# First output projection of a hybrid decoder layer: the last two weight blocks taken tile by tile, its norm split in two steps, and the sample attention spread over another stretch

## The chip, the cores and the metric

One core of one Trainium2 chip runs the kernel; the seven others are idle. The metric is the device time of one execution in microseconds (us), as the median of several runs. Five engines work side by side, each through its own list of instructions in a fixed order: PE (TensorE, matmuls and transposes), DVE (VectorE), ACT (ScalarE), POOL (GpSimd) and SP (SyncE, which here only issues DMAs). An engine stops at an instruction whose inputs are not ready, and all that stands behind it in its list stops with it.

## What is computed

One layer of a hybrid decoder, for a prompt of 1024 tokens and for 8 samples of 8 new tokens over a paged cache of 512 positions. The model width is 1024, the feed-forward width 2816, and everything is float32.

```python
xn = rmsnorm(x, norm_mix_g)
z = xn @ w_in                       # columns of four head groups
mix = concatenate([y_lru, y_sc, y_fox, y_diff]) @ w_out
x = x + mix                         # "first output projection"
x = x + (silu(rmsnorm(x) @ w_gate) * (rmsnorm(x) @ w_up)) @ w_down
y = rmsnorm(x, norm_final_g)        # at the very end
```

`y_fox` is a forgetting attention and `y_diff` a differential attention (two softmaxes, the second subtracted with a weight lambda, then a norm over each head). For the samples both run over gathered cache pages plus the new rows. The change touches the multiplication by `w_out` for the first 512 prompt tokens, the RMSNorm behind it, and the order in which the sample attention is laid beside them.

## The kernel before

**Precision.** Every float32 product is made of three matmuls (`mm3`, L94 to L97): each operand is split into a high part and the rest, `whi` and `wlo` for a weight, `xTh` and `xTl` for an activation. A weight block of 1 MB is loaded by SP into a `raw` tile (a ring of three) and split in four parts of 128x512, each part by one ACT copy (`whi`, L326) and one DVE subtraction (`wlo`, L327), into a ring of eight pairs of tiles. `W.get` (L369) asks for a block and, while `W.ahead` is set, also starts the split of the next one, as far as the ring has room.

**Order of the work.** The program is a list of items, each a cost and a function that emits instructions. `merge(a, b, frac)` (L1255) interleaves two lists so that the share of cost done in both stays equal; with `frac` below 1 the second list is used up when that share of the first is done. The items are emitted in that order; the tile scheduler then sets the order on each engine and may place an instruction ahead of others that were emitted before it. `keep` (L86) marks an instruction as one to be kept in program order.

**The stage around the change** (about 340 to 500 us of the span). The first half of the prompt (four tiles of 128 tokens) has its mixed rows in `xTh`, `xTl`. `w_out_items` (L1596) multiplies them with `w_out` in four column blocks of 256: for block n, for each tile t, 24 matmuls of 256 columns into one of three `pb_mm` banks, then a DVE addition to the residual `acc[t]` (L1611). So the order is block by block, tile inside. `load_acc` (L1864) loads the four residual tiles of 512 KB each from the input with SP (L1869). Behind the projection `norm2_items` (L1876) runs `norm_T` (L440) on each tile: ACT squares and sums the row (`rstd_of`, L431), DVE makes one over the root from nine small operations (L433, L123, and three times L125 and L126), scales the tile into a `raw` tile (L443), PE transposes it in two lots of four (L450, banks `pb_t`, of which there are two), and ACT and DVE write the halves `xTh` (L452) and `xTl` (L453). The `raw` tile comes from the same ring of three as the weight blocks. Then the gate and up matmuls of the first feed-forward blocks run, merged with the second half's attention (`att_items`), which `att1_open` (L2011 to L2030) opens with its loads `aqt`, `afb`, `akt`, `avt`.

**The sample attention** (`sample_items`, L1341) is a second list, merged with the projection: 60% of its items over the projection behind its first items, the other 40% over the norm. In two groups (fox) and four groups (diff) it does: gather of K pages by POOL (`spgk`, L1406) and transposes (`kT`, L1424, copies L1426 and L1428), scores (`qk`, L1439), softmax on DVE and ACT (L1464 to L1482), transposes of the probabilities (`pT`, L1493, L1496, copies L1494, L1497), the product with V (`pv`, L1507, L1512, gathered `spgv`), a masked product that selects the rows (`som`, `sel`, L1522, L1526), and after each group kind `fin` (L1535 to L1556): for diff a sum (L1532), square, reduction and a root of some dozen small DVE operations, a scaling (L1548), and two transposes (L1551) whose results go to `syt` (L1554). `setup_c` (L1362) loads the constants `sc` and computes from them `ssg` (L1373), a 128x1 weight for diff's softmax; `setup_b` loads `sbias` and `snb`, from which POOL makes the bias (L1464).

The lines of the program that order all this are L2138 to L2150. In the changed kernel the same code stands some lines lower: L1373 is L1395, L1611 is L1616, L443 is L442, L450 is L453, L452 and L453 are L455 and L456, L1526 is L1531, L1548 is L1553, L1551 is L1556, L1554 is L1559, L1058 is L1064.

Of the kernel before, what the change touches and what calls it, by code (L numbers as in the profile page):

```python
# [8 lines left out]
F32 = mybir.dt.float32  # L9
# [32 lines left out]
P3_FRAC = .75  # L42
P3_SMP = 0.6
N1_FRAC = 0.6
# [21 lines left out]
def hybrid_step(ctx, tc, I, C, O):  # L66
# [370 lines left out]

    st_x = {}

    def norm_T(pool, x, gb, R, xh, xl, c0, act=False):  # L440
        xs = big(pool, "nxs", 2)[:R]
        y = rstd_of(x, xs, R, "n", act)  # L442
        st_x["x"] = nc.vector.scalar_tensor_tensor(xs, x, y[:R], gb[:R], op0=OP.mult, op1=OP.mult)  # L443
        kn = 512 // R
        for kk in range(8 // kn):
            pt = bank("t")
            pv = pt.rearrange("p (k r) -> p k r", r=R)
            for i in range(kn):
                k = kk * kn + i
                nc.tensor.transpose(pv[:, i, :], xs[:, k * 128:(k + 1) * 128], ident[:R, :R])  # L450
            ks = slice(kk * kn, (kk + 1) * kn)
            nc.scalar.activation(xh[:, ks, c0:c0 + R], pv, AF.Copy)  # L452
            nc.vector.tensor_tensor(xl[:, ks, c0:c0 + R], pv, xh[:, ks, c0:c0 + R].bitcast(F32), op=OP.subtract)  # L453
        if R == 64:
            nc.vector.tensor_copy(xh[:, :, c0 + 64:c0 + 128], xl[:, :, c0:c0 + 64].bitcast(F32))  # L455

    def xT_tiles(pool, smp):
# [883 lines left out]
    def sample_items(E_):  # L1341
# [20 lines left out]
        def setup_c():  # L1362
            sp = E_["sp"]
            t = sp.tile(list(CN["smp"].shape), F32, name="sc")
            nc.sync.dma_start(t, C["smp"])
            c = 0
            for nm, nf, nd in (("bm", 4, 4), ("sel", 128, 256), ("msk", 128, 256)):
                for key, n in (("f", nf), ("d", nd)):
                    S[nm + key] = t[:, c:c + n]
                    c += n  # L1370
            S["sgA"], S["sgB"] = t[:, c:c + 1], t[:, c + 1:c + 2]
            sg = sp.tile([128, 1], F32, name="ssg")
            nc.vector.scalar_tensor_tensor(sg, S["sgB"], nlam, S["sgA"], op0=OP.mult, op1=OP.add)  # L1373
            S["sg"] = sg
        def setup_b():
# [13 lines left out]
        def setup_d():  # L1389
            setup(False)  # L1390
            bd = S["bd"]
            S["bo"] = bo = E_["hp"].tile([128, 576], F32, name="sbo", tag="hTl", bufs=3)[:, :520]
# [203 lines left out]
    def w_out_items(hf, e):  # L1596
        items = []

# [16 lines left out]
        for n in range(4):  # L1615
            r = [f(n, t, c, kind) for t, c, kind in tok_tiles(hf)]  # L1616
            if hf == 0 and n == 0:
                items += sum((x[:3] for x in r[:3]), []) + sum((x[3:] for x in r[:3]), [])
                r = r[3:]
            items += sum(r, [])  # L1620
        return items

# [241 lines left out]
    def load_acc(pool, hf):  # L1864
        acc = []
        for t in range(4 + hf):
            a = pool.tile([128, D], F32, name=f"acc{t}")
            if t < 4:
                nc.sync.dma_start(a, I["x_prompt"][0, hf * HALF + t * 128:hf * HALF + (t + 1) * 128, :])  # L1869
            else:  # L1870
                nc.vector.memset(a[64:128], 0.0)
                nc.sync.dma_start(a[0:64], I["x_sample"].rearrange("s t d -> (s t) d"))
            acc.append(a)
        return acc

    def norm2_items(hf, e):  # L1876
        st = {}

        def f(t):
# [11 lines left out]
            return g  # L1891
        return [(900, f(t)) for t in range(4 + hf)]

    def final_items(hf, e):
# [82 lines left out]
    def do(f):  # L1977
        return [(0, f)]
# [164 lines left out]
    smp = SM_ITEMS[3:]  # L2143
    k = int(len(smp) * P3_SMP)
    wo = w_out_items(0, E2[0])
    prog += SM_ITEMS[:3] + wo[:WO_HEAD] + merge(wo[WO_HEAD:], smp[:k]) + merge(norm2_items(0, E2[0]), smp[k:]) + do(att1_open)
    prog += merge(head, att_items(A1, 1), P3_FRAC)
# [94 lines left out]
```

## Time and profile before

| | |
|---|---|
| median of 3 runs | 1378.14 us (1369.75 to 1383.42) |
| the profiled execution | 1374.64 us |
| its span, first to last instruction | 1372.9 us |
| PE busy | 1342.1 us (98%) |
| DVE busy | 1058.3 us (77%) |
| ACT busy | 675.7 us (49%) |
| mean DMA rate | 148 GB/s |
| mean granted PE clock | 0.993 |

The profile is of one execution; the span leaves out 1.7 us of it before the first and behind the last instruction. "Idle before" an instruction is the time its engine stood still, with what released it. A row with xN at the end is N instructions in one line.

### The profile page before, as it was taken

The numbers are of one execution on the slowest core, as the hardware profiler recorded it, in microseconds if no ns is written. First come the engines' busy times: TensorE is split into PE (matmuls) and PEld (weight loads), VectorE is DVE, ScalarE is ACT, GpSimd is POOL, SyncE is SP. The second block draws the span as 40 slices with busy tenths as digits, with TensorE's granted clock in tenths as the row PEclk, the third lists the DMA queues.
The fourth block names the chain that finished last, engine by engine and source line by source line (L and its number), as shares of the span: only waits on it lengthen the run. The fifth ranks groups of instructions, "written<-read, shape, count | busy, mean of one in ns | idle before, by whom it ended". The sixth has DMA issues, their size and how long they took to land.

```text
span 1372.9 us, 23083 instructions
## 1 busy us (share of the span) xinstructions
PE 1342.1 (98%) x8477; PEld 1182.0 (86%) x8477; DVE 1058.3 (77%) x2699; ACT 675.7 (49%) x1326; POOL 125.1 (9%) x154
## 2 busy tenths in 40 slices
PE   9899999999899999999999999999999999999997
PEld 8799897888786688888888999997999999999996
DVE  6776377798446568899969988548998888888885
ACT  6585466775233258655544444324534444444454
POOL 3101012311243011000000000000200000000001
PEclk9999999999999999999999999999999999999999
DMA  8656438676994376444236433612624333333311
GB/s 259 203 169 206 139 118 274 211 229 217 328 305 152 108 238 196 147 131 124 86 116 190 123 92 93 192 48 62 200 62 123 93 92 93 93 92 93 93 47 69
DMA packets 202866, 202.65 MB, mean 148 GB/s; under 512 B 16529, under 2 KB 165549, under 8 KB 202626
## 3 DMA queue, kind: packets, MB, share of 16 engines
q1 hardware_dynamic: 189568, 168.60, 40.3%
q0 software_dynamic: 7328, 25.11, 5.2%
q10 hardware_dynamic: 5858, 7.47, 1.5%
q8 instruction: 67, 1.10, 0.3%
q14 instruction: 45, 0.37, 0.1%
HBM read 170.56 MB, written 32.29 MB: 148 GB/s over the span
## 4 chain that ended last, share of the span: by engine, by line
PE 81%; DMA 7%; ACT 5%; DVE 4%; issue 1%; SPq 0%; POOL 0%; ACTq 0%; DVEq 0%; POOLq 0%
PE pb_mm L95 10%; PE pb_mm L96 10%; PE pb_mm L97 10%; PE pb_mm L1746 8%; PE pb_s L1746 5%; PE pb_t L1746 5%; PE pb_o L1162 2%; PE pb_t L95 2%; PE pb_s L97 2%; PE pb_t L96 2%; PE pb_o L1746 2%; PE pb_s L96 2%; PE pb_s L95 2%; PE pb_t L97 2%; PE pb_t L1142 2%; DMA raw<-in_w_in_dram 2%
## 5 line engine op out<-in xcount | busy, mean ns | idle before, releaser
L326 ACT ACTIVATE whi<-raw 128x512 fp32r<-128x512 f32 (+1 forms) x409 | 251.8, 629 | 353.1 <-PE pb_mm L97 75.6
L327 DVE TENSOR_TENSOR wlo<-raw,whi 128x512 fp32r<-128x512 f32 (+1 forms) x405 | 275.8, 692 | 71.6 <-ACT whi L326 62.9
L95 PE MATMUL pb_mm<-xTh,whi 128*128 128x512 f32 (+2 forms) x536 | 192.5, 359 | 1.7 <-ACT whi L326 1.5
L96 PE MATMUL pb_mm<-xTl,whi 128*128 128x512 f32 (+2 forms) x536 | 191.1, 357 | 0.3 <-DVE xTl L453 0.3
L97 PE MATMUL pb_mm<-xTh,wlo 128*128 128x512 f32 (+2 forms) x536 | 190.7, 356 | 0.3 <-DVE wlo L327 0.3
L97 PEld LDWEIGHTS pb_mm<-xTh,wlo 128*128 128x128 f32 x536 | 101.1, 189 | 13.9 <-issue 1.6
L95 PEld LDWEIGHTS pb_mm<-xTh,whi 128*128 128x128 f32 x536 | 101.2, 189 | 13.7 <-ACT whi L326 1.7
L96 PEld LDWEIGHTS pb_mm<-xTl,whi 128*128 128x128 f32 x536 | 101.3, 189 | 10.4 <-DVE xTl L453 0.5
L95 PE MATMUL pb_mm<-whi,xTh 128*128 128x256 f32 (+1 forms) x312 | 92.1, 295 | 4.9 <-DVE acc L1611 4.9
L96 PE MATMUL pb_mm<-wlo,xTh 128*128 128x256 f32 (+1 forms) x312 | 89.3, 286 | 0.0
L97 PE MATMUL pb_mm<-whi,xTl 128*128 128x256 f32 (+1 forms) x312 | 89.1, 286 | 0.0
L1100 ACT ACTIVATE aP<-aP,anm 128x128 f32<-128x128 f32 (+7 forms) x96 | 73.9, 770 | 30.0 <-DVE anm L1098 28.6
L1832 DVE TENSOR_TENSOR acc<-acc,pb_mm 128x512 f32<-128x512 f32 (+1 forms) x95 | 64.7, 681 | 15.1 <-PE pb_mm L97 13.2
L95 PE MATMUL pb_mm<-whi,hTh 128*128 128x512 f32 (+1 forms) x179 | 70.7, 395 | 0.1
L97 PE MATMUL pb_mm<-whi,hTl 128*128 128x512 f32 (+1 forms) x179 | 70.6, 394 | 0.0
L96 PE MATMUL pb_mm<-wlo,hTh 128*128 128x512 f32 (+1 forms) x179 | 70.3, 393 | 0.0
L95 PEld LDWEIGHTS pb_mm<-whi,xTh 128*128 128x128 f32 x312 | 60.0, 192 | 10.1 <-DVE acc L1611 5.1
L97 PEld LDWEIGHTS pb_mm<-whi,xTl 128*128 128x128 f32 x312 | 59.9, 192 | 0.6 <-issue 0.4
L96 PEld LDWEIGHTS pb_mm<-wlo,xTh 128*128 128x128 f32 x312 | 60.1, 193 | 0.4 <-DVE wlo L327 0.2
L1147 DVE TENSOR_TENSOR aAl<-pb_t,aAh 128x512 fp32r<-128x512 f32 (+1 forms) x80 | 49.1, 632 | 6.0 <-ACT aAh L1146 5.0
L1746 PE MATMUL pb_mm<-xTh,whi 128*128 128x288 f32 (+1 forms) x184 | 53.7, 292 | 0.0
L1746 PE MATMUL pb_mm<-xTh,wlo 128*128 128x288 f32 (+1 forms) x184 | 53.7, 292 | 0.0
(623 smaller groups left out, 3773.2 us busy)
## 6 DMA issues: line engine op xcount, KB each, us to landing
raw<-in_w_gate_dram SPq DMA_DIRECT2D x44, 512.0 KB
raw<-in_w_up_dram SPq DMA_DIRECT2D x44, 512.0 KB
raw<-in_w_down_dram SPq DMA_DIRECT2D x22, 1024.0 KB
raw<-in_w_in_dram SPq DMA_DIRECT2D x12, 1024.0 KB
raw<-in_w_in_dram SPq DMA_DIRECT2D x16, 512.0 KB
raw<-in_w_out_dram SPq DMA_DIRECT2D x8, 1024.0 KB
akt<-fkD SPq DMA_DIRECT2D x24, 256.0 KB
akt<-dkD SPq DMA_DIRECT2D x48, 128.0 KB
```

Of the source, the lines that this page charges most:

```text
L95: kp(nc.tensor.matmul(out, lhsT=lh, rhs=rh, start=first, stop=False))
L96: kp(nc.tensor.matmul(out, lhsT=lh, rhs=rl, start=False, stop=False))
L97: kp(nc.tensor.matmul(out, lhsT=ll, rhs=rh, start=False, stop=last))
L326: i1 = nc.scalar.activation(hi, s, AF.Copy)
L327: i2 = (nc.gpsimd if pool else nc.vector).tensor_tensor(lo, s, hi.bitcast(F32), op=OP.subtract)
L1100: nc.scalar.activation(dst[:, :ln], dst[:, :ln], AF.Exp, bias=nmx, accum_out=sm)
L1142: nc.tensor.transpose(pt[:, o:o + 128], P[ti][:, kb * 128:(kb + 1) * 128], ident)
L1147: nc.vector.tensor_tensor(al[:, :o], pt[:, :o], ah[:, :o].bitcast(F32), op=OP.subtract)
L1162: nc.tensor.matmul(po[:, q0:q0 + n], lhsT=v[:, kb, :], rhs=a[:, o:o + n], start=kb == 0 and i == 0, stop=kb >= nkb - 2 and i == 1, skip_gr ...
L1746: nc.tensor.matmul(pt, lhsT=w[:, k], rhs=x[:, k], start=first and k == 0 and i == 0, stop=k == 3 and i == 2, skip_group_check=True)
L1832: nc.vector.tensor_tensor(a, a, pt, op=OP.add)
```

## The change

Six things are done, all in the stage described.

1. `norm_T` is divided into `norm_a` (square, root, scaling, on ACT and DVE) and `norm_b` (transposes and copies).
2. Of the projection's four column blocks the first two stay as they were. The last two (`w2`, `w3`) are both kept split in the ring of eight and are taken tile by tile: tile 0 of both, then tile 1, and so on. After each tile its `norm_a` is emitted, and from tile 2 on `norm_b` of the tile two before. `W.ahead` is off meanwhile; the first gate and up block is split (`split_next`) in tile 3 between its two blocks.
3. `norm_b` of tiles 2 and 3 is emitted after the first gate and the first up group of the feed-forward; these two groups leave the list that is merged with the second half's attention.
4. The sample items are merged with the whole of this by 0.8: they are all emitted when eight tenths of its cost is.
5. `ssg` is computed in `setup_d` (the start of the diff groups), marked with `keep`, instead of in `setup_c`.
6. The four residual tiles are loaded in two column pieces each, first 256 columns of all four, then 768: eight DMAs instead of four.

```diff
-    def norm_T(pool, x, gb, R, xh, xl, c0, act=False):
+    def norm_a(pool, x, gb, R, act=False):
         xs = big(pool, "nxs", 2)[:R]
         y = rstd_of(x, xs, R, "n", act)
-        st_x["x"] = nc.vector.scalar_tensor_tensor(xs, x, y[:R], gb[:R], op0=OP.mult, op1=OP.mult)
+        nc.vector.scalar_tensor_tensor(xs, x, y[:R], gb[:R], op0=OP.mult, op1=OP.mult)
+        return xs
+    def norm_b(xs, R, xh, xl, c0):
...
         def setup_c():
...
-            sg = sp.tile([128, 1], F32, name="ssg")
-            nc.vector.scalar_tensor_tensor(sg, S["sgB"], nlam, S["sgA"], op0=OP.mult, op1=OP.add)
-            S["sg"] = sg
         def setup_d():
             setup(False)
+            sg = S["sg"] = E_["sp"].tile([128, 1], F32, name="ssg")
+            keep(nc.vector.scalar_tensor_tensor(sg, S["sgB"], nlam, S["sgA"], op0=OP.mult, op1=OP.add))
...
     def w_out_items(hf, e):
-        items = []
+        items, late = [], []
...
-            items += sum(r, [])
-        return items
+            if hf == 0 and n >= 2:
+                late.append(r)
+            else:
+                items += sum(r, [])
+        return (items, late) if hf == 0 else items
...
     def load_acc(pool, hf):
-        acc = []
-        for t in range(4 + hf):
-            a = pool.tile([128, D], F32, name=f"acc{t}")
...
+        acc = [pool.tile([128, D], F32, name=f"acc{t}") for t in range(4 + hf)]
+        for w in (slice(0, D),) if hf else (slice(0, 256), slice(256, D)):
+            for t in range(4):
+                nc.sync.dma_start(acc[t][:, w], I["x_prompt"][0, hf * HALF + t * 128:hf * HALF + (t + 1) * 128, w])
...
+    def norm2_steps(e):
+        st = {}
+        def a(t):
+            def f():
+                if t == 0:
+                    st["g"] = gload(None, I["norm_ffn_g"])
+                st[t] = norm_a(None, e["acc"][t], st["g"], 128)
+            return f
+        def b(t):
+            def f():
+                norm_b(st[t], 128, e["xh"], e["xl"], t * 128)
+            return f
+        return [(a(t), b(t)) for t in range(4)]
...
     smp = SM_ITEMS[3:]
-    k = int(len(smp) * P3_SMP)
-    wo = w_out_items(0, E2[0])
-    prog += SM_ITEMS[:3] + wo[:WO_HEAD] + merge(wo[WO_HEAD:], smp[:k]) + merge(norm2_items(0, E2[0]), smp[k:]) + do(att1_open)
+    wo, (w2, w3) = w_out_items(0, E2[0])
+    nrm2 = norm2_steps(E2[0])
+    def split_next():
+        i = widx["gu", 0, 0]
+        W.split_to(i, 4)
+    rows = do(lambda: setattr(W, "ahead", False))
+    for t in range(4):
+        rows += w2[t] + (do(split_next) if t == 3 else []) + w3[t] + do(nrm2[t][0])
+        if t >= 2:
+            rows.append((430, nrm2[t - 2][1]))
+    prog += SM_ITEMS[:3] + wo[:WO_HEAD] + merge(wo[WO_HEAD:] + rows, smp, SMP_FRAC) + do(lambda: setattr(W, "ahead", True))
+    prog += head[:NP_F] + [(430, nrm2[2][1])] + head[NP_F:2 * NP_F] + [(430, nrm2[3][1])] + do(att1_open)
+    head = head[2 * NP_F:]
     prog += merge(head, att_items(A1, 1), P3_FRAC)
```

The order on the engines is shown at three places. The first is DVE where `ssg` stands, while the first two column blocks of the projection run (`acc` is the residual, `sc` the constants, `wlo` the rest of a split weight). Before:

```order
L1611 TENSOR_TENSOR acc1_4831<-acc1_4831,pb_mm_4911 128x256
L1611 TENSOR_TENSOR acc2_4833<-acc2_4833,pb_mm_4930 128x256
L1373 SCALAR_TENSOR_TENSOR ssg_5146<-sc_5144,nlam_71 128x1
L327 TENSOR_TENSOR wlo_5000<-raw_4875,whi_4999 128x512
L327 TENSOR_TENSOR wlo_5004<-raw_4875,whi_5003 128x512
L327 TENSOR_TENSOR wlo_5008<-raw_4875,whi_5007 128x512
L1611 TENSOR_TENSOR acc3_4835<-acc3_4835,pb_mm_4970 128x256
L327 TENSOR_TENSOR wlo_5012<-raw_4875,whi_5011 128x512
```

After:

```order
L1616 TENSOR_TENSOR acc1_4830<-acc1_4830,pb_mm_4915 128x256
L1616 TENSOR_TENSOR acc2_4831<-acc2_4831,pb_mm_4934 128x256
L1395 SCALAR_TENSOR_TENSOR ssg_5355<-sc_5128,nlam_71 128x1
L327 TENSOR_TENSOR wlo_5004<-raw_4879,whi_5003 128x512
L327 TENSOR_TENSOR wlo_5008<-raw_4879,whi_5007 128x512
L327 TENSOR_TENSOR wlo_5012<-raw_4879,whi_5011 128x512
L1616 TENSOR_TENSOR acc3_4832<-acc3_4832,pb_mm_4974 128x256
L327 TENSOR_TENSOR wlo_5016<-raw_4879,whi_5015 128x512
```

`ssg` has another line number and comes from a later item, and stands at the same place: behind the third tile's addition, ahead of the three `wlo` and the fourth tile's addition. Nothing has moved here.

The second place is ACT at the end of the projection in the changed kernel, where the squares of the norm (L431) stand among the splits of the first two gate and up blocks (`raw_5299` and `raw_5443`; the squares write `raw_5572` and `raw_5767`, tiles of the same ring of three).

```order
L326 ACTIVATE whi_6041<-raw_5299 128x512
L326 ACTIVATE whi_6045<-raw_5299 128x512
L326 ACTIVATE whi_6049<-raw_5299 128x512
L326 ACTIVATE whi_6053<-raw_5299 128x512
L326 ACTIVATE whi_6116<-raw_5443 128x512
L431 ACTIVATE raw_5572,nss_5573<-acc0_4829 128x1024
L326 ACTIVATE whi_6120<-raw_5443 128x512
L326 ACTIVATE whi_6124<-raw_5443 128x512
L326 ACTIVATE whi_6128<-raw_5443 128x512
L431 ACTIVATE raw_5767,nss_5768<-acc1_4830 128x1024
L455 ACTIVATE xTh_4626<-pb_t_5956 128x4x128
L431 ACTIVATE raw_5941,nss_5942<-acc2_4831 128x1024
```

Of the kernel before, the same engine around its first square:

```order
L326 ACTIVATE whi_5516<-raw_5225 128x512
L326 ACTIVATE whi_5520<-raw_5225 128x512
L326 ACTIVATE whi_5524<-raw_5225 128x512
L326 ACTIVATE whi_5528<-raw_5225 128x512
L1426 ACTIVATE skT_5540<-pb_t_5541 128x512
L431 ACTIVATE raw_5768,nss_5769<-acc0_4829 128x1024
L1477 ACTIVATE sP_5587,ssm_5595<-sP_5587,snm_5593 128x576
```

In both, the first square stands behind all four splits of the first gate and up block. After the change that block is the one whose split waits for the third column block's tile 3: its ring tiles hold the third block until then. So the square of tile 0 is behind the product of tile 3 with the third block, and the square of tile 1 behind the second block's splits, which wait for the fourth block's tile 3. The square of tile 0 also takes the `raw` tile that the first block's last `wlo` sets free.

The third place is PE at the end of the projection (`raw` is the normed tile, `som` and `syd` belong to the sample attention's last selection and its end). Before, from the row behind the projection's last product on:

```order
L1526 MATMUL pb_t<-som,sc 64x256
L450 MATMUL pb_t<-ident,raw 128x128 x8
L1439 MATMUL pb_t<-zS_dk_87,sqbd_5428 32x64 x2
L1439 MATMUL pb_t<-zS_dk_88,sqbd_5434 32x64 x2
L1424 MATMUL pb_t<-ident,spgk 128x128 x8
L1439 MATMUL pb_s<-skT,sqbd_5428 32x512
L1493 MATMUL pb_t<-ident,sP 128x128 x4
L1496 MATMUL pb_t<-ident,sP 64x128
L450 MATMUL pb_t<-ident,raw 128x128 x3
L1507 MATMUL pb_o<-vS_d,sPT 128x256
L1512 MATMUL pb_o<-spgv,sPT 64x256 x8
L450 MATMUL pb_t<-ident,raw 128x128 x5
```

After, from its last products to the first gate products:

```order
L95 MATMUL pb_mm<-whi,xTh 128x256
L96 MATMUL pb_mm<-wlo,xTh 128x256
L97 MATMUL pb_mm<-whi,xTl 128x256
L453 MATMUL pb_t<-ident,raw 128x128 x8
L1531 MATMUL pb_t<-som,sc 64x256
L1556 MATMUL pb_t<-ident,syd 128x64 x2
L453 MATMUL pb_t<-ident,raw 128x128 x8
L95 MATMUL pb_mm<-xTh,whi 128x256 x2
L96 MATMUL pb_mm<-xTl,whi 128x256
L97 MATMUL pb_mm<-xTh,wlo 128x256
L95 MATMUL pb_mm<-xTh,whi 128x256
```

Before, the norm's transposes stand among the sample attention's last two groups; a single last selection and its end come later among gate and up products. After, the transposes of tiles 0 and 1, the last selection and the two transposes of its end stand in one row, with no product of the projection or of the feed-forward between them. DVE's order there is: scaling of tile 0, root and scaling of tile 1, `xTl` of tile 0, then the end of the diff groups (from the sum L1537 to the scaling L1553) with the root and scaling of tile 2 among it.

## Rows read from the trace of the kernel before

**Rows 1.** The page: busy time (us, share, instructions) and the chain that ended last.

```profile
PE 1342.1 (98%) x8477; PEld 1182.0 (86%) x8477; DVE 1058.3 (77%) x2699; ACT 675.7 (49%) x1326; POOL 125.1 (9%) x154
...
PE 81%; DMA 7%; ACT 5%; DVE 4%; issue 1%; SPq 0%; POOL 0%; ACTq 0%; DVEq 0%; POOLq 0%
```

**Rows 2.** Windows (us): length, busy by engine (x instructions), PE clock, DMA share, GB/s.

```profile
370.00:380.00 10.00, 5.14 (x31) 4.94 (x31) 3.62 (x8) 0.60 (x1) 2.18 (x3) 0.74 1.08 273
380.00:390.00 10.00, 10.00 (x92) 8.21 (x91) 4.79 (x12) 3.30 (x7) 5.38 (x8) 0.92 1.08 366
...
430.00:440.00 10.00, 9.13 (x71) 6.47 (x68) 6.36 (x13) 4.52 (x8) 2.99 (x3) 1.00 0.49 159
440.00:450.00 10.00, 7.47 (x38) 3.80 (x39) 7.94 (x29) 3.00 (x7) 0.00 (x0) 0.83 0.01 2
450.00:460.00 10.00, 9.53 (x62) 5.88 (x61) 7.10 (x23) 4.02 (x8) 0.94 (x1) 1.00 0.17 52
...
470.00:480.00 10.00, 9.42 (x68) 6.37 (x68) 6.15 (x18) 3.34 (x7) 0.00 (x0) 1.00 0.41 114
```

**Rows 3.** Timeline of PE, 371 to 377 us: start, duration, instruction [idle before].

```profile
371.44 0.28 PE L96 MATMUL pb_mm<-wlo,xTh 128*128 128x256 f32 x1
371.56 0.28 PE L97 MATMUL pb_mm<-whi,xTl 128*128 128x256 f32 x1
376.70 0.58 PE L95 MATMUL pb_mm<-whi,xTh 128*128 128x256 f32 x1 [4.86 <-DVE acc L1611]
```

**Rows 4.** Timeline of DVE, 366 to 377 us (columns as above).

```profile
366.18 0.42 DVE L1611 TENSOR_TENSOR acc<-acc,pb_mm 128x256 f32<-128x256 f32 x1 [3.04 <-DMA acc<-in_x_prompt_dram]
374.29 0.22 DVE L1373 SCALAR_TENSOR_TENSOR ssg<-sc,nlam 128x1 f32<-128x1 f32 x1 [7.69 <-DMA sc<-c_smp_dram]
374.42 1.89 DVE L327 TENSOR_TENSOR wlo<-raw,whi 128x512 fp32r<-128x512 f32 x3
```

**Rows 5.** Timeline of SP's queue, the load of the constants.

```profile
366.77 0.33 SPq L1365 DMA_DIRECT2D sc<-c_smp_dram  x1
```

**Rows 6.** Groups by line, 340 to 500 us: busy, mean ns of one | idle before.

```profile
L327 DVE TENSOR_TENSOR wlo<-raw,whi 128x512 fp32r<-128x512 f32 x30 | 20.4, 692 | 13.8 <-ACT whi L326 13.5
...
L326 ACT ACTIVATE whi<-raw 128x512 fp32r<-128x512 f32 x30 | 18.7, 630 | 31.9 <-PE pb_mm L97 17.9 <-PE pb_mm L96 11.6 <-DMA xTh<-yD 1.5
...
L443 DVE SCALAR_TENSOR_TENSOR raw<-acc,nry,raw 128x1024 f32<-128x1024 f32 x4 | 5.1, 1282 | 0.1
...
L452 ACT ACTIVATE xTh<-pb_t 128x512 fp32r<-128x512 f32 x8 | 4.6, 595 | 18.8 <-PE pb_t L450 18.8
...
L431 ACT ACTIVATE raw<-acc 128x1024 f32<-128x1024 f32 x4 | 4.2, 1054 | 3.7 <-DVE acc L1611 3.7
...
L125 DVE TENSOR_SCALAR nrs_z<-nms,nry 128x1 f32<-128x1 f32 x12 | 3.3, 273 | 0.3
```

**Rows 7.** Timeline of PE in the norm and the sample attention's last groups.

```profile
436.92 0.65 PE L1526 MATMUL pb_t<-som,sc 128*64 128x256 f32 x2
437.50 0.66 PE L450 MATMUL pb_t<-ident,raw 128*128 128x128 f32 x4
...
443.05 1.91 PE L1439 MATMUL pb_s<-skT,sqbd 128*32 128x512 f32 x2 [1.50 <-ACT skT L1426]
...
445.81 0.42 PE L1496 MATMUL pb_t<-ident,sP 128*64 128x128 f32 x1
...
447.27 0.70 PE L1507 MATMUL pb_o<-vS_d,sPT 64*128 64x256 f32 x2
```

**Rows 8.** Timeline of DVE at the end of the diff groups.

```profile
479.98 0.41 DVE L1532 TENSOR_TENSOR syd<-syd,pb_t 64x256 f32<-64x256 f32 x1
...
486.97 0.41 DVE L1548 TENSOR_TENSOR syd<-syd,sry 64x256 f32<-64x256 f32 x1
```

**Rows 9.** Timeline of SP's queue, the first loads of the second attention's keys.

```profile
487.22 3.38 SPq L1010 DMA_DIRECT2D akt<-fkD  x4
```

**Rows 10.** Timeline of PE, the second attention's first scores.

```profile
498.98 0.33 PE L1058 MATMUL pb_s<-akt,aqt 128*128 128x384 f32 x1
```

More of the change, by code (lines that the diff above doesn't have):

```diff
@@ L42 @@
 P3_FRAC = .75
-P3_SMP = 0.6
+SMP_FRAC = 0.8
 N1_FRAC = 0.6
@@ L436, in rstd_of @@
         return y
-    st_x = {}
-    def norm_T(pool, x, gb, R, xh, xl, c0, act=False):
+    def norm_a(pool, x, gb, R, act=False):
         xs = big(pool, "nxs", 2)[:R]
         y = rstd_of(x, xs, R, "n", act)
-        st_x["x"] = nc.vector.scalar_tensor_tensor(xs, x, y[:R], gb[:R], op0=OP.mult, op1=OP.mult)
+        nc.vector.scalar_tensor_tensor(xs, x, y[:R], gb[:R], op0=OP.mult, op1=OP.mult)
+        return xs
+    def norm_b(xs, R, xh, xl, c0):
         kn = 512 // R
@@ L455, in norm_T @@
             nc.vector.tensor_copy(xh[:, :, c0 + 64:c0 + 128], xl[:, :, c0:c0 + 64].bitcast(F32))
+    def norm_T(pool, x, gb, R, xh, xl, c0, act=False):
+        norm_b(norm_a(pool, x, gb, R, act), R, xh, xl, c0)
     def xT_tiles(pool, smp):
@@ L1864, in load_acc @@
     def load_acc(pool, hf):
-        acc = []
-        for t in range(4 + hf):
-            a = pool.tile([128, D], F32, name=f"acc{t}")
[L1868 to L1873, printed above, removed]
+        acc = [pool.tile([128, D], F32, name=f"acc{t}") for t in range(4 + hf)]
+        for w in (slice(0, D),) if hf else (slice(0, 256), slice(256, D)):
+            for t in range(4):
+                nc.sync.dma_start(acc[t][:, w], I["x_prompt"][0, hf * HALF + t * 128:hf * HALF + (t + 1) * 128, w])
+        if hf:
+            nc.vector.memset(acc[4][64:128], 0.0)
+            nc.sync.dma_start(acc[4][0:64], I["x_sample"].rearrange("s t d -> (s t) d"))
         return acc
```

## The prediction

> **What bounds the kernel now.** I read the page first: PE is busy 98% of the span and holds 81% of the chain that ended last [rows 1]. So the time falls only where PE now stands or runs at the lower clock, and rises where PE gets a new wait. Next I read the windows over the stage that the change touches [rows 2]. PE loses 4.86 us in 370 to 380, and in 430 to 480, where the norm runs, it loses 0.87 + 2.53 + 0.47 + 0.58 = 4.45 us (10 less its busy time; 460 to 470 is full and has no row). The granted clock falls to 0.74 and 0.92 behind the first loss and to 0.83 in 440 to 450. A mean of 0.83 between the levels 2.4 and 1.2 GHz means 3.4 of the 10 us at the lower one, which is about 1.7 us of lost work. Everywhere else in the stage PE is nearly full. The timelines then say who holds PE. In the first place it waits for an addition to the residual that frees a bank [rows 3]. That addition is late because DVE's list has `ssg` ahead of it, and `ssg` stands 7.69 us for the load of the constants [rows 4]. In the second place the norm's chain of ACT and DVE steps and the sample attention's steps take turns [rows 7].
>
> **The change part by part.** The matmuls, the splits and the norm's instructions are the same in number. New are four DMA issues, so the sum is made of waits alone. It is made against the profiled execution, 1374.64 us, which lies 3.5 us below the median of 1378.14.
>
> *`ssg` and the wait behind it: 0.* In the order of the changed program `ssg` stands at the same place on DVE, between the same two additions, and still reads the constants. The load was issued at 366.77 [rows 5] and DVE went on at 374.29 [rows 4]. The same bytes of the residual lie ahead of it in SP's list, in eight pieces for four, and the issue is held by an earlier store, not by them. The wait for the third tile's residual, 3.04 us at 366.18 [rows 4], can shorten, as its first 256 columns are asked for earlier; but DVE then stands at `ssg` all the sooner, and PE's bank is freed by the addition behind it. I take 0. The ends are -5 us, if the load lands as much earlier as PE waited [rows 3], and +1 us.
>
> *The sample attention's chains among the products: +2.* At their tightest places the scores, transposes and products with V of one group now have 2 to 4 products between them where there were 6 to 18. A step with too little between shows its price in the rows of before: PE waited 1.50 us for a copy ahead of scores [rows 7]; from the start of the last transposes to the product with V it took 447.27 - 445.81 = 1.46 us, of which a fill of three products and one score covers about 0.6 us and the transpose 0.4, so some 0.5 is left. Three of the six products with V stand so close and five scores have two products (0.24 us) ahead of a copy of 0.6 us. That is 3 x 0.5 + 5 x 0.4 = 3.5 us. Of what such places cost before, 1.50 us is in the 4.45 above, which is subtracted as a whole below; against it some of the new waits can fall together, so I take 2. The ends are 0 and 5.
>
> *The end of the projection: +11.5.* The title says two tiles behind, and the order says otherwise. The square of tile 0 stands on ACT behind the split of the first gate and up block, whose tiles hold the third column block until tile 3 has used it. Count from the end of tile 3's last product with the third block. The fourth block's 24 products, whose starts lie 0.12 us apart [rows 3], end PE's work at 2.8 us. Meanwhile: one split on ACT and DVE 0.63 + 0.69, the square 1.05 and some 0.2 to read its sum out, to 2.7. Then DVE does nine small operations of some 0.2 us each (1.9 in all; L125, the longest kind, takes 0.27), an addition 0.42 [rows 4], three `wlo` that stand among them (2.0) and the scaling of 1.28 [rows 6]. That is 8.3 us, so PE stands 5.5 us. It transposes tile 0 in about 0.8 (four took 0.66, of which the last's end overlaps with what follows [rows 7]). The next row, the last selection, needs the `pb_t` bank that `xTl` of tile 0 frees, and DVE has the root (1.9) and scaling (1.28) of tile 1 ahead of it: 12.2 us, another 3.1 us of standing. Behind the selection (0.6 of its 0.65 [rows 7]) come the two transposes of the end. They wait for the whole end of the diff groups, which takes from 479.98 to 486.97, 7.0 us, in the run of before, with other work among it [rows 8]. Here it has four operations of 0.41, twelve small ones, and six small ones and a scaling for tile 2 among it: 6.7 us, another 7.1 us of standing with the `xTl` ahead of it. Then 0.5 us for the copies that free the bank, tile 1's transposes 0.8, and 0.9 and 0.6 us until both halves of its `xTh` and `xTl` are there, the second behind a square. Together PE stands 17.7 us. Before, the stretch lost 4.45 us by standing and about 1.7 by the clock. The difference is 17.7 - 6.15 = 11.5 us. Before, the same end of the diff groups lay under gate and up products and cost nothing; that cover is gone. The ends are 5 us (if the small operations overlap and only half of the stops stays) and 15 us (all of it, and the gate's first products at the lower clock).
>
> What the clock adds is seen in rows: behind the stop of 4.86 us the first product took 0.58 us [rows 3], and the next ten us had 0.92 [rows 2]. The Trainium skill, in "TensorE: Matmul & The Clock Gate" (Why this matters for your kernels), says that idle gaps between bursts of matmuls bring the slow clock back; the trace of before agrees at 370 and at 440 us. By that rule each of the three stops would bring it back, and the end would lie at 15, not at 11.5.
>
> *Loads of the second attention: 0.* The second half's first scores ran at 498.98 [rows 10], 11.8 us after the issue of the first keys [rows 9]. In the new order SP issues these behind the third gate and up block, whose `raw` tile is free only when tile 2 is transposed, and the first scores come about 11 us after the first gate product. That is close; I take 0, with 3 at the upper end.
>
> Sum: 0 + 2 + 11.5 + 0 = 13.5 us, 1374.64 + 13.5 = 1388 us.
>
> **Rivals.** *The load of the constants lands earlier.* With the first columns of all four residual tiles in front, the queue could run emptier, and PE's 4.86 us [rows 3] would go: 1388 - 5 = 1383. For it speaks that the load is a small one that took 7.5 us; against it that the bytes ahead of it are the same.
>
> *The clock stays low and the keys come late.* If every stop brings the lower level back, the selection, the transposes and the first gate products run at half speed, and the first scores wait too: 2 + 15 + 3 = 20, 1395 us. For it speak the 0.74 and 0.83 [rows 2], after single stops shorter than two of the three here; against it that little lies between the stops.
>
> *The norm really runs ahead (the other side).* If the square of tile 0 is done while the projection still has work, the roots and scalings of tiles 0 and 1 lie under products of the projection. Then only the end of the diff groups is left, and a part of it is covered too. PE would stand some 2 us where it lost 6.15: 1374.64 - 4 + 2 of the chains = 1372 us, and 1367 if `ssg` also gives 5. It decides at one place: whether the square of tile 0 starts before tile 3's last product with the third block. For it speaks that tile 0's sums are complete some 14 us earlier (120 products, 0.12 us apart, lie between); against it the order, in which its `raw` tile is the one that the last split part frees.
>
> *The change doesn't do what it says* is part of the forecast itself, in two points: `ssg` does not move, and the norm does not run two tiles behind.
>
> **How the numbers follow.** Forecast 1388: 0.52. Constants earlier, 1383: 0.15. Clock and keys, 1395: 0.25. Norm ahead, 1367 to 1372: 0.08. The range for eight in ten goes from 1374 (most of the norm-ahead case left out; the sum with both lower ends, -5 + 0 + 5, gives 1375) to 1400 (a little over 1395; the sum with all upper ends, 1 + 5 + 15 + 3, gives 1399). A measurement of this kernel can tell about 1% from no change, 13.8 us, and the forecast lies just there: I give slower by over 1% 0.42 (half of the bulk near 1388 and most of the third case), within 1% 0.53, faster by over 1% 0.05 (the norm-ahead case with more gained elsewhere).
>
> **What would show it.** Right: DVE's `ssg` still stands some 7 us for `sc`, PE about 5 us for the addition behind it; the square of tile 0 starts after tile 3's last product with the third block; PE stands about 5, 3 and 7 us ahead of tile 0's transposes, the last selection and the transposes of `syd`; the first gate product starts some 20 us behind the last product of the projection. Wrong: no stop of PE over 2 us in that row, or `ssg` without a wait. If the stops are there and the time is the same, something that I count as full before was not.

## The result, and the profile after

The changed kernel takes 1390.72 us (median of 4 runs, 1387.7 to 1393.56) beside 1375.09 us for the kernel before (the median with a fourth run added to the three of the table); the ratio is 1.0112, with a 95% interval of 1.0074 to 1.015. That is some 15 us more, a little over the 1% that the prediction named as the least that a measurement can tell. The profiled execution took 1391.87 us, its span 1390.1 us.

The page of the changed kernel, busy time and chain, answers to [rows 1]:

```profile
PE 1347.7 (97%) x8477; PEld 1185.0 (85%) x8477; DVE 1057.6 (76%) x2699; ACT 676.8 (49%) x1326; POOL 126.5 (9%) x154
...
PE 81%; DMA 6%; DVE 5%; ACT 5%; issue 2%; SPq 0%; ACTq 0%; POOL 0%; DVEq 0%; POOLq 0%
```

PE is busy 5.6 us longer in a span that is 17.2 us longer, so in these two executions most of the loss is standing, and a part of it is matmuls that take longer. The share of the chain on PE is the same, and nothing on the page says where. The windows do (length, busy by engine, granted clock, DMA share, GB/s; [rows 2] of before):

```profile
360.00:370.00 10.00, 7.34 (x41) 7.14 (x41) 1.80 (x4) 3.10 (x10) 2.67 (x4) 0.68 0.88 296
370.00:380.00 10.00, 10.00 (x85) 10.00 (x85) 4.13 (x9) 2.57 (x5) 3.46 (x5) 0.98 0.94 285
...
390.00:400.00 10.00, 8.57 (x83) 5.37 (x83) 4.89 (x10) 4.10 (x6) 4.67 (x5) 1.00 1.05 387
...
450.00:460.00 10.00, 10.00 (x76) 7.12 (x76) 5.95 (x16) 2.81 (x6) 0.00 (x0) 1.00 0.00 0
460.00:470.00 10.00, 5.28 (x39) 4.71 (x36) 8.10 (x24) 5.28 (x10) 0.00 (x0) 0.80 0.00 0
470.00:480.00 10.00, 2.61 (x10) 1.23 (x9) 8.66 (x32) 2.34 (x5) 0.01 (x1) 0.50 0.00 0
480.00:490.00 10.00, 9.77 (x69) 9.11 (x68) 5.95 (x15) 4.07 (x8) 1.78 (x4) 0.84 0.20 57
```

From 460 to 480 us PE is busy 7.89 of 20 us, and 0.50 means that it had the lower of its two levels (1.2 and 2.4 GHz) all through 470 to 480. DVE is the busiest engine there. The stop of 4.86 us at 371 of before is not in this execution; 2.66 us are lost in 360 to 370 and 1.43 us in 390 to 400. The timeline of PE at the end of the projection (start, duration, instruction, and in brackets the idle time before it with what ended it):

```profile
461.00 0.28 PE L95 MATMUL pb_mm<-whi,xTh 128*128 128x256 f32 x1
...
463.73 0.28 PE L97 MATMUL pb_mm<-whi,xTl 128*128 128x256 f32 x1
468.73 1.94 PE L453 MATMUL pb_t<-ident,raw 128*128 128x128 f32 x8 [4.72 <-DVE nms L433]
472.32 1.11 PE L1531 MATMUL pb_t<-som,sc 128*64 128x256 f32 x2 [1.65 <-DVE nms L433]
478.91 0.45 PE L1556 MATMUL pb_t<-ident,syd 64*128 64x64 f32 x2 [5.47 <-DVE syd L1553]
479.62 1.97 PE L453 MATMUL pb_t<-ident,raw 128*128 128x128 f32 x8 [0.27 <-DVE syt L1559]
481.43 0.80 PE L95 MATMUL pb_mm<-xTh,whi 128*128 128x256 f32 x2
```

Between the projection's last product at 463.73 and the first gate product at 481.43 there is no product, and PE stops three times: 4.72, 1.65 and 5.47 us. ACT and DVE at the same time:

```profile
462.60 1.06 ACT L431 ACTIVATE raw<-acc 128x1024 f32<-128x1024 f32 x1
...
466.91 1.06 ACT L431 ACTIVATE raw<-acc 128x1024 f32<-128x1024 f32 x1 [1.61 <-DVE wlo L327]
```

```profile
467.29 1.29 DVE L442 SCALAR_TENSOR_TENSOR raw<-acc,nry,raw 128x1024 f32<-128x1024 f32 x1
...
470.38 1.28 DVE L442 SCALAR_TENSOR_TENSOR raw<-acc,nry,raw 128x1024 f32<-128x1024 f32 x1
471.58 0.68 DVE L456 TENSOR_TENSOR xTl<-pb_t,xTh 128x512 fp32r<-128x512 f32 x1
...
473.47 0.41 DVE L1537 TENSOR_TENSOR syd<-syd,pb_t 64x256 f32<-64x256 f32 x1 [0.16 <-PE pb_t L1531]
...
475.45 1.28 DVE L442 SCALAR_TENSOR_TENSOR raw<-acc,nry,raw 128x1024 f32<-128x1024 f32 x1
...
478.34 0.42 DVE L1553 TENSOR_TENSOR syd<-syd,sry 64x256 f32<-64x256 f32 x1
```

The square of tile 0 starts at 462.60, behind tile 3's last product with the third block (that is the one before 461.00). DVE's six rows are the steps PE waits for, in order: tile 0 scaled, tile 1 scaled, the `xTl` that frees the bank, then the sum, tile 2's scaling in between, and the scaling of `syd`. The trace names `nms` (L433) as what ended the first two stops. That is a small operation of the next tile's root, which starts just as the scaling or the `xTl` ends (468.50, 472.18), and the transposes don't read it; that the step ahead of it is what PE needed is inferred from the program.

The place of `ssg`, for [rows 4], and the place that stopped PE instead:

```profile
370.04 0.42 DVE L1616 TENSOR_TENSOR acc<-acc,pb_mm 128x256 f32<-128x256 f32 x1 [0.86 <-PE pb_mm L97]
374.88 0.22 DVE L1395 SCALAR_TENSOR_TENSOR ssg<-sc,nlam 128x1 f32<-128x1 f32 x1 [4.42 <-DMA sc<-c_smp_dram]
```

```profile
360.36 0.31 ACTq L954 DMA_DIRECT2D out_p_lru_h_dram<-go  x1
362.94 0.25 ACTq L954 DMA_DIRECT2D out_p_lru_conv_dram<-go  x1
...
363.75 0.60 ACT L1431 ACTIVATE skT<-pb_t 128x512 f32<-128x512 f32 x1 [4.72 <-DMA acc<-in_x_prompt_dram]
```

```profile
364.41 1.11 PE L1429 MATMUL pb_t<-ident,spgk 128*128 128x128 f32 x4 [2.66 <-ACT skT L1431]
```

DVE stands at `ssg` again, 4.42 us for the constants. PE does not, as it came late: ACT stood between two issues of output stores until 362.94 (the trace names a load of the residual as what ended it, in the third row), made the copy of the keys behind them at 363.75, and PE's next transposes waited 2.66 us for that copy.

### The profile page after: what moved, and what is told of

Its sections match the earlier page's. It is cut to its first block, busy times and chain, and to the rows that moved or that the text cites. A ratio compares the mean times of both kernels' runs of the same rounds, so it can differ in the third digit from the quotient of the medians.

```text
span 1390.1 us, 23081 instructions
## 1 busy us (share of the span) xinstructions
PE 1347.7 (97%) x8477; PEld 1185.0 (85%) x8477; DVE 1057.6 (76%) x2699; ACT 676.8 (49%) x1326; POOL 126.5 (9%) x154
## 4 chain that ended last, share of the span: by engine, by line
PE 81%; DMA 6%; DVE 5%; ACT 5%; issue 2%; SPq 0%; ACTq 0%; POOL 0%; DVEq 0%; POOLq 0%
PE pb_mm L95 11%; PE pb_mm L96 10%; PE pb_mm L97 10%; PE pb_mm L1754 8%; PE pb_s L1754 5%; PE pb_t L1754 5%; PE pb_o L1168 2%; PE pb_s L97 2%; PE pb_s L96 2%; PE pb_s L95 2%; PE pb_t L95 2%; PE pb_o L1754 2%; PE pb_t L97 2%; PE pb_t L96 2%; PE pb_t L1148 2%
## 5 line engine op out<-in xcount | busy, mean ns | idle before, releaser
L1152 ACT ACTIVATE aAh<-pb_t 128x512 fp32r<-128x512 f32 (+1 forms) x80 | 42.5, 550 | 28.2 <-PE pb_t L1148 24.5
```

The lines of the kernel that those rows point to most:

```text
L1152: nc.scalar.activation(ah[:, :o], pt[:, :o], AF.Copy)
```

## The experiments

Three questions were open: whether the three stops are the loss and the norm's late start and the end of the diff groups their causes; what `ssg` and the loads are worth; and whether the density of the sample attention counts. Each kernel was timed in five rounds beside the kernel before; ratios are to it, with the interval in brackets. A difference between two such ratios carries both intervals: for 1.0112 less 1.005 it is 0.6%, within 0.2 to 1.0%.

**The end of the diff groups later.** One item is taken out of the merge and put behind the first two feed-forward groups.

```diff
-merge(wo[WO_HEAD:] + rows, smp, SMP_FRAC)
+merge(wo[WO_HEAD:] + rows, smp[:-1], SMP_FRAC)
-head[NP_F:2 * NP_F] + [(430, nrm2[3][1])]
+head[NP_F:2 * NP_F] + smp[-1:] + [(430, nrm2[3][1])]
```

> The changed kernel with one item moved: the end of the diff groups (square, root, scaling of syd, its two transposes) is emitted behind the first gate and up groups instead of among the projection's rows. Theory (three stops of PE at the end of the projection, each waiting for DVE): the stop of 5.5 us ahead of the two transposes of syd goes, the stops ahead of tile 0's transposes (4.7 us) and of the last selection (1.7 us) stay, and with the stop some of the time at the lower clock goes: 6 to 9 us faster than the changed kernel, ratio to before about 1.005. Rival (the stops are only where PE waits for the norm of tile 1 anyway): tile 1's transposes or the first gate product take over the wait and no more than 2 us are won, ratio 1.010.

Measured: 1386.29 us, 1.005 (1.0032 to 1.0068). PE's rows at that place:

```profile
467.47 1.94 PE L453 MATMUL pb_t<-ident,raw 128*128 128x128 f32 x8 [4.76 <-DVE nms L433]
471.06 1.11 PE L1531 MATMUL pb_t<-som,sc 128*64 128x256 f32 x2 [1.65 <-DVE nms L433]
...
483.70 0.31 PE L1556 MATMUL pb_t<-ident,syd 64*128 64x64 f32 x2 [1.50 <-DVE syd L1553]
```

The first two stops are as they were, the third is 1.50 us instead of 5.47, now behind gate products. This agrees with the theory: some 8.5 us (1.0112 less 1.005) for 4 us of standing. The rest can be the clock: it was 0.83, 0.66 and 1.00 in 460 to 490, which makes 10 of these 30 us at the lower level, where the changed kernel's 0.80, 0.50 and 0.84 make 17.

**A ring tile kept free.** While the projection's last block is fetched, one block ahead is loaded instead of two.

```diff
-            self.load_to(i + 3)
+            self.load_to(i + (2 if self.specs[i][0] == ("wo", 0, 3) else 3))
```

> The changed kernel, except that with the projection's last block only one block ahead is loaded, so that one tile of the raw ring is free when tile 0's sums are complete. Theory (tile 0's square waits for the ring tile that the last split part of the first gate and up block frees): the square of tile 0 starts some 10 us or more ahead of tile 3's last product with the third block, the stops ahead of tile 0's transposes (4.7 us) and of the last selection (1.7 us) go, the one ahead of the transposes of syd stays at 4 to 7 us: 6 to 8 us faster than the changed kernel, ratio to before about 1.005. Rival (the chain of root and scaling is late on DVE and ACT for other reasons, the copies and splits ahead of it): the square comes earlier, yet tile 0's transposes still wait over 3 us, ratio 1.010.

Measured: 1386.71 us, 1.0055 (1.0035 to 1.0074). First ACT's square of tile 0, then PE at the end of the projection:

```profile
423.42 1.06 ACT L431 ACTIVATE raw<-acc 128x1024 f32<-128x1024 f32 x1 [1.11 <-DVE acc L1616]
```

```profile
462.94 0.44 PE L453 MATMUL pb_t<-ident,raw 128*128 128x128 f32 x2
...
467.68 0.65 PE L1531 MATMUL pb_t<-som,sc 128*64 128x256 f32 x2
...
477.19 0.45 PE L1556 MATMUL pb_t<-ident,syd 64*128 64x64 f32 x2 [6.30 <-DVE syd L1553]
```

The square starts at 423 us, some 40 us earlier. Tile 0's transposes and the last selection have no wait before them any more, and the stop ahead of the transposes of `syd` is still there with 6.30 us. So the late start came from the ring tile, and the rival, other work on ACT and DVE, falls.

**Both edits.**

> Both edits of the two runs beside it in one kernel. Theory: all three stops go but for 1 to 3 us ahead of tile 1's transposes or the first gate product, the granted clock stays above 0.95 at the end of the projection, 13 to 16 us faster than the changed kernel, ratio to before 0.998 to 1.002. Rival (another wait takes over, as the gate needs both tiles' halves): a stop of over 5 us remains there, ratio above 1.004.

Measured: 1381.25 us, 1.002 (1.0002 to 1.0038). PE at tile 1's transposes and at the end of the diff groups:

```profile
460.88 1.90 PE L453 MATMUL pb_t<-ident,raw 128*128 128x128 f32 x8 [2.19 <-DVE sms L1550]
...
470.58 0.31 PE L1556 MATMUL pb_t<-ident,syd 64*128 64x64 f32 x2 [0.20 <-DVE syd L1553]
471.21 1.09 PE L453 MATMUL pb_t<-ident,raw 128*128 128x128 f32 x8 [0.32 <-DVE syt L1559]
473.72 0.74 PE L95 MATMUL pb_mm<-xTh,whi 128*128 128x256 f32 x3 [1.43 <-ACT xTh L455]
```

One stop of 2.19 and one of 1.43 us are left (behind the first the clock was 0.83 in 460 to 470, below the 0.95 expected). Together the edits give back 1.0112 - 1.002 = 0.9%, some 13 of the 15 us (7 to 18 with both intervals); the ratio is at the upper end of what was expected. The row at 471.21 also gives the clock's price: eight transposes in 1.09 us here, at a granted clock of 1.00, and in 1.97 us in the row at 479.62 of the changed kernel, at 0.50.

**The residual loaded whole.**

```diff
-        for w in (slice(0, D),) if hf else (slice(0, 256), slice(256, D)):
+        for w in (slice(0, D),):
```

> The changed kernel with the four residual tiles loaded whole, as before the change. Theory (the four added loads change which DMA waits for which: ACT's output stores wait for a piece of the residual, the copy behind them is late and PE stands 2.7 us for it at the start of the projection; ssg's wait for the constants is as long as before but PE meets it later): the 2.7 us stop goes and a stop of 3 to 5 us behind ssg comes back, within 3 us of the changed kernel. Rival (the pieces are a gain, as the additions wait less): 4 us or more slower than the changed kernel. Second rival (the pieces are a pure loss): 3 us or more faster.

Measured: 1393.52 us, 1.0124 (1.0092 to 1.0156), not told apart from the changed kernel. So no gain or loss of the pieces is seen; one of 5 us would fit in the two intervals. The detail of the theory was only half right: in its profile the wait for the copy of the keys shrinks to 1.36 us, but does not go, the addition stops PE for 1.61 us, and a stop of 4.40 us comes in, behind the first softmax of the sample attention (`smx`). The three stops at the end of the projection are the same to the hundredth, in another execution:

```profile
467.32 1.94 PE L453 MATMUL pb_t<-ident,raw 128*128 128x128 f32 x8 [4.72 <-DVE nms L433]
470.92 1.12 PE L1531 MATMUL pb_t<-som,sc 128*64 128x256 f32 x2 [1.65 <-DVE nms L433]
477.50 0.45 PE L1556 MATMUL pb_t<-ident,syd 64*128 64x64 f32 x2 [5.47 <-DVE syd L1553]
```

**`ssg` on POOL, in the kernel before.**

```diff
-            nc.vector.scalar_tensor_tensor(sg, S["sgB"], nlam, S["sgA"], op0=OP.mult, op1=OP.add)
+            nc.gpsimd.tensor_tensor(sg, S["sgB"], nlam, op=OP.mult)
+            nc.gpsimd.tensor_tensor(sg, sg, S["sgA"], op=OP.add)
```

> The kernel before the change with ssg computed by POOL (a product and a sum) instead of by one DVE operation, so that DVE no longer stands for the constants. Theory (this wait was the cause of PE's stop of 4.9 us before, and the change left it in place): the stop behind the additions to the residual goes; what is late next is the softmax's bias, which waits for its own loads, and takes part of it back: 2 to 6 us faster than before, ratio 0.996 to 0.998. Rival (PE would have waited at that place for its loads anyway): a stop of 4 us or more appears within the next 20 us, ratio 0.999 to 1.001.

Measured: 1371.62 us, 0.9972 (0.9948 to 0.9997): faster than before by some 4 us. PE's longest waits, 345 to 520 us (what waited, for what: us in total, times, longest):

```profile
PE pb_t L1425 <- ACT skT L1427: 1.8, 1, 1.8
PE pb_s L1440 <- ACT skT L1427: 1.5, 1, 1.5
```

The 4.86 us for the addition [rows 3] are gone; the longest wait is now the 1.8 us for the copy of the keys. So about that much the move of `ssg` could have given, had it moved the instruction. This kernel loads the residual whole, and so did the one with 1.36 us there: the pieces don't cause that wait.

**Two parts of the change alone, in the kernel before**: `ssg` in `setup_d` with `keep`, and the residual in pieces (the hunks of the change, no others).

> The kernel before with two parts of the change alone: ssg computed in setup_d and marked with keep, and the four residual tiles loaded in two pieces each. Theory (ssg stands at the same place in DVE's order and waits as long, and the pieces only shift which DMA waits for which): DVE still stands 4 us or more at ssg, ratio to before 0.998 to 1.003. Rival (these two parts cost some of the loss): ratio 1.004 or more. Second rival (they are worth what they seem to be meant for): ratio 0.997 or less.

Measured: 1374.33 us, 0.9996 (0.9974 to 1.0018): no difference seen. DVE's row:

```profile
374.57 0.22 DVE L1389 SCALAR_TENSOR_TENSOR ssg<-sc,nlam 128x1 f32<-128x1 f32 x1 [3.50 <-DMA sc<-c_smp_dram]
```

It stands 3.50 us, less than the 4 us expected, and starts at nearly the same time as before, 374.57 beside 374.29: the additions ahead of it had come later. In this execution PE does not stand for the additions, but 2.54 us for the copy of the keys.

**The changed kernel's sample items spread wider**, 1.1 for 0.8 and nothing else.

```diff
-SMP_FRAC = 0.8
+SMP_FRAC = 1.1
```

> The changed kernel with nothing but 1.1 for 0.8: the sample items last to the end of the projection's rows and a little beyond. Theory (the three stops of 12 us together come from the norm's late start, and the end of the diff groups stays among them; sample steps between them cover a part): 2 to 6 us faster than the changed kernel, ratio 1.006 to 1.010. Rival (the density of the sample attention is the main cause of the loss): 10 us or more faster, ratio 1.004 or less. Second rival (it plays no part): ratio 1.011 to 1.013.

Measured: 1388.35 us, 1.012 (1.0092 to 1.0147): the second rival. The stop at `syd` shrinks to 0.6 us, those ahead of tile 0's transposes (4.6) and of the last selection (1.6) stay, and new stops of 3.4 us (in two) ahead of the transposes of probabilities and of 1.3 us ahead of a norm transpose come in, so it moves the loss and does little to lower it.

**The same on top of both edits, and with `ssg` on POOL.**

> The changed kernel with the ring tile kept free and the end of the diff groups moved behind the first gate and up groups (the two edits that were run together), and the sample items spread to the end of the projection's rows and a little beyond (1.1 for 0.8). Theory (the sample attention's steps and the norm's steps cover each other when they lie together, and the denser sample attention meets its bias and its pages too early): the stops at 375 to 392 us and at the norm both shrink, 3 to 6 us faster than with 0.8, ratio to before 0.996 to 0.999. Rival (density does not matter): same as with 0.8, ratio 1.001 to 1.003.

Measured: 1378.93 us, 1.005 (1.0024 to 1.0076), against expectation no better than with 0.8, and above the rival's range too.

```profile
PE pb_t L1556 <- DVE syd L1553: 5.4, 1, 5.4
```

The stop at the end of the diff groups is back with 5.4 us: in PE's order 16 products now lie between the last selection and those transposes, where over 60 lay.

> As the kernel with 1.1 beside it, with ssg computed by POOL. Theory: DVE no longer stands for the constants; where PE stood for it the stop goes, 0 to 4 us faster than the kernel beside it, ratio to before 0.993 to 0.998. Rival (in the changed kernel PE no longer waits there): no difference to the kernel beside it.

Measured, with `ssg` on POOL too: 1378.67 us, 1.0034 (1.0011 to 1.0057), not told apart from the kernel beside it: the rival.

> The changed kernel with the ring tile kept free, the end of the diff groups behind the first gate and up groups, and ssg computed by POOL, sample items by 0.8. Theory: the stops at the end of the projection are gone as without the third edit; PE in the changed kernel does not stand for ssg but for the bias and the pages of the dense sample attention, so POOL's part gives less than the 3.6 us that it gave the kernel before: ratio 0.999 to 1.002. Rival (ssg is worth as much here): ratio 0.996 to 0.998, which would be as good as the kernel before with ssg on POOL.

Measured, with 0.8: 1377.44 us, 1.0033 (1.0011 to 1.0055), not told apart from the 1.002 without POOL, and short of the range expected. In the profile of the changed kernel `ssg` is not what PE waits for, which fits that freeing DVE of it gave nothing.

**The sample attention taken from the norm, in the kernel before.**

```diff
-P3_SMP = 0.6
+P3_SMP = 0.9
```

> The kernel before with 90% of the sample items over the projection instead of 60%, and so 10% over the norm. Theory (before, the norm's steps cost so little because the sample attention's last two groups lay among them; with these gone PE stands for the root and scaling of each tile): PE stands 8 us or more at the norm where it stood 4.5 us, 4 to 9 us slower than before, ratio 1.003 to 1.007. Rival (gate and up products cover the norm as well): ratio 0.998 to 1.002.

Measured: 1377.97 us, 1.0029 (1.0006 to 1.0052), just below what was expected; so is the standing. PE in the norm, two windows and its longest stop:

```profile
450.00:460.00 10.00, 5.49 (x41) 3.05 (x39) 8.69 (x26) 5.85 (x12) 0.00 (x0) 0.96 0.00 0
460.00:470.00 10.00, 7.86 (x31) 4.32 (x31) 3.81 (x12) 0.57 (x2) 0.00 (x0) 0.53 0.00 0
```

```profile
461.12 1.09 PE L1493 MATMUL pb_t<-ident,sP 128*128 128x128 f32 x4 [4.80 <-DVE sP L1482]
```

From 430 to 490 PE stands 7.35 us (60 less 52.65 busy) where it stood 4.45 and 8 were expected. The longest stop is not one for the norm's own steps but for a softmax that has DVE's norm steps ahead of it: here the two streams cover each other only as long as both have work.

**The copies of the keys on DVE, in the kernel before with `ssg` on POOL.**

```diff
-                    if pr == 0:
+                    if pr == 0 and (key == "d" or s > 1):
                         nc.scalar.activation(kT[:, pr, :], pt, AF.Copy)
```

> The kernel before with ssg on POOL, and with the first two key copies of the sample attention on DVE, where ACT made them behind six issues of output stores. Theory (in the run with ssg on POOL PE's longest stop was the 1.8 us for such a copy, and ACT made it late because it stood at a store's issue): that stop goes and DVE, which is idle there, makes the copies at once: 1 to 4 us faster than with ssg on POOL alone, ratio to before 0.994 to 0.997. Rival (PE arrives earlier at the additions to the residual and stands there for the loads): no difference, ratio 0.997 to 0.999.

Measured: 1371.97 us, 0.9981 (0.9955 to 1.0006). PE's wait of 1.8 us for these copies is gone from the profile (the one of 1.5 us is for a later copy, and stays), and the time is not told apart from that of the kernel with `ssg` on POOL alone: the rival. Of all versions, `ssg` on POOL alone is the one that beats both kernels with its whole interval, if by little.

## Why the prediction was right

The prediction said 1388 us, between 1374 and 1400; measured were 1390.72. Of its three classes it held "within 1%" the likeliest (0.53) and "slower by over 1%" less so (0.42); 1.0112 is the latter, with an interval that reaches into the former. Step by step:

*The end of the projection, +11.5.* Right in its cause, shown by the two edits that give back 0.9% together (13 us, 7 to 18). That the size came out as well is in part luck, as its parts were off in opposite directions. I counted 17.7 us of standing; the three stops and the two small ones behind them (0.27 and 0.23) are 12.3 us. Two things make the difference. The chain of steps was shorter: from tile 3's last product with the third block, about 461.2, to the first gate product it took 20.2 us where my steps add up to 22.7. And PE's own rows in it took longer, at the lower clock, which I had left for the upper end: 1.94 and 1.97 us for eight transposes that I had counted at 0.8, and 1.11 for the selection that I had counted at 0.6. The granted clock was 0.80, 0.50 and 0.84 in 460 to 490. The Trainium skill's rule that idle gaps between bursts of matmuls bring the slow clock back ("TensorE: Matmul & The Clock Gate", Why this matters for your kernels) agrees with these rows. Behind short stops it is less sure: at 440 us the kernel before had 0.83 behind stops of at most 1.50 us, and two of its variants (`ssg` on POOL, and the two parts alone) had 1.00 behind stops of the same kind and length. The case "the clock stays low" was right as to the clock, and its keys came late by only 0.8 us.

By rows the sum doesn't close. PE's standing there grows by 7.9 us (12.3 less 4.45), and the transposes and the selection take 2.3 us more than the same rows at a clock of 1.00, of which the kernel before lost a part too: some 10 us of the 15. In the two profiles another 2 us of standing lie ahead of 340 us, before the stage begins (14.79 beside 12.65 us). Where the rest went was not found.

*The chains of the sample attention, +2.* Wrong as worked out: at such places PE waited 0.15 us in the execution profiled. I had the cover too small. In the changed kernel the step from the last transposes to the product with V, with three products and one score between, looks so:

```profile
404.91 0.27 PE L1501 MATMUL pb_t<-ident,sP 128*64 128x128 f32 x1
...
405.48 1.05 PE L1444 MATMUL pb_s<-skT,sqbd 128*32 128x512 f32 x2
406.45 0.70 PE L1512 MATMUL pb_o<-vS_f,sPT 64*128 64x256 f32 x2
```

It takes 1.54 us, about the 1.46 of before, and PE doesn't stand: the score alone fills 0.97 us from start to start, where I had put the score and the three products at 0.6 together. And the 1.50 us for a copy ahead of scores was not the price of few products alone: ACT made that copy late, at 442.42, behind two squares of the norm (439.58 and 440.62) and a row of the softmax. But the denser sample attention is not shown to be free. In four other profiles with this 0.8 (the kernels with the late end, the free ring tile, both, and whole loads) PE stood 3.98, 4.87, 2.76 and 4.40 us behind the first softmax (`smx`). With the ring tile free, DVE's row and then PE's:

```profile
390.40 0.22 DVE L1478 CUSTOM_DVE_ANT_0 sP<-pb_t,sbias 128x64 f32<-128x64 f32 x1 [5.14 <-remote]
```

```profile
390.69 1.12 PE L1429 MATMUL pb_t<-ident,spgk 128*128 128x128 f32 x4 [4.87 <-DVE smx L1478]
```

The trace doesn't name what DVE waited for ("remote"). The profiles of the changed kernel itself, of both edits with `ssg` on POOL, of the kernel before and its variants, and of those with 1.1 don't have this stop. What it adds to the medians is not known; with 1.1 alone the changed kernel's time was the same.

*`ssg`, 0.* Right in sum: the parts alone give 0.9996, and whole loads make no difference that is seen. Right too that `ssg` waits at the same place in DVE's order, though 4.42 us where I said some 7, as DVE came to it later. Its load, called a small one in the rival, moves 389 KB, beside 512 KB for a tile of the residual; the time of that rival, 1383, did not come. That PE would stand 5 us behind it was wrong for the execution profiled: it stood 2.66 us earlier for a copy, and 1.43 us for pages; that this is nearly the same sum (4.09 for 4.86) is luck. In the executions profiled of kernels built from the changed one, the stops from 355 to 400 us fall in different places; those at the end of the projection don't, unless an edit moves them.

*The loads of the second attention, 0.* Right: 0.76 us ahead of the first scores.

The other side, the norm running ahead, turned on whether the square starts before tile 3's last product with the third block. It starts behind it. With a ring tile free it starts 40 us earlier and the norm does run ahead. That case had the time fall below that of before, and this it doesn't do: 1.0055 with this edit, 1.002 with both. PE's waits from 345 to 520 us, summed over the view of waits, are 13.0 us in the kernel with both edits and 9.7 in the one before: the 3 us between them are about the 0.2% that is left, spread over copies, pages, a softmax and keys. As each is one execution and these stops move about, which of them is the cause stays open.

## What to carry to other kernels

A step that is emitted earlier is not done earlier when its tile comes from a ring that the work ahead of it still holds: look for the tile's last reader before counting on a lead. The chain of small operations at the end of the diff groups cost next to nothing under matmuls and 5 to 6 us without them, and the transposes that followed ran at the lower clock as well. And read the compiled order for the one instruction that was to move; here it had not moved, and putting it on another engine won some 4 us.

## What the runs showed that was not expected

Short rows between stops ran at the lower clock throughout: eight transposes took 1.94 and 1.97 us for 1.09, and the last selection 1.11 for 0.65. And an engine that only issues a store can hold up a copy behind it: ACT stood 2.3 us between two issues (360.36 with 0.31 to 362.94), and PE stood 2.66 us for the copy that came next.
